# Turning softmax rows: from TensorE transposes to 32x32 block transposes on VectorE and a pass through DRAM

## The chip, the cores and the metric

The kernel runs on one core of a Trainium2 chip. A core has TensorE (PE, with its weight loads shown as PEld), VectorE (DVE), ScalarE (ACT), GpSimd (POOL) and SyncE (SP), which here only issues DMAs. Each engine works through its own instruction list in order; between engines there are only semaphores. The metric is the device time of one execution in microseconds (us): the median of the runs. One execution was also profiled, and its trace is what the views below are taken from.

## What is computed

One layer of a bidirectional encoder block, for 256 positions and a model width of 2048, in float32:

```
xn = rms_norm(x, norm_pre_w);  z = xn @ w_in
u, g_lru, q, k, v, g_attn, m_lru, m_attn = split(z)
u   = centred_depthwise_conv(u)                      # width 4
h   = rg_lru(u, forward) + rg_lru(u, backward)       # gates, decays, scans
y_a = h * silu(g_lru)
q, k = partial_rope(q), partial_rope(k)
y_b = windowed_gqa(q, k, v, sink) * silu(g_attn)     # 16 heads, 4 key/value heads, |i-j| <= 128
merged = sigmoid(m_lru) * (y_a @ w_proj_a) + sigmoid(m_attn) * (y_b @ w_proj_b)
out = x + rms_norm(merged @ w_out, norm_post_w)
```

The change touches the attention. For a head, `p = softmax(q k^T + mask, with a sink)` is a 256 x 256 matrix. It is made with the queries on the partitions, since the sums run over the keys; the product `p @ v` contracts over the keys, so TensorE wants p with the keys on the partitions. Each head's p must be turned.

## The kernel before

**Matmuls.** Every float32 factor is split into a high part (a cast to fp32r, on ScalarE) and a low part (the rest, a subtraction on VectorE); a product is three fp32r matmuls, high x high, high x low and low x high (`mm3`, lines 223 to 227). `parts_of` (line 147) does that split for activations, `split` (line 209) for weights.

**Weights and half-steps.** `START`, `MERGE` and `OUT` (lines 57 to 68) write out by hand in which order the weight blocks are used: 182 steps, each with a load of 2048 columns, treated in two halves. The loop at the end (line 1121) goes through them. Time in the program is counted in half-steps ("ticks"): a block of kind `blk` or `quad` takes two, a `part` (of the seven-product scheme `Seven`) one. One half-step is about 2.7 us of matmuls. At a step the load three steps ahead is issued on SP into one of three `raw` buffers (`fetch`, line 201, issue on line 207); at a half the weights four halves ahead are split (lines 217 to 221). All else is hung into this order by `at(tick, function)` and `soon(function)`, which is "one half-step later"; the functions due at a half-step are emitted before its matmuls. So on each engine work of the weights and work of the heads stand in one list, in the order of half-steps.

**What else SP issues.** Finished units that are not needed for a while are parked in DRAM (`park`, line 792, issue on line 797) and brought back (`back`, line 799, issue on line 801); the sums of the seven-product scheme are stored (line 335) and loaded (line 340); first cells of accumulated weights are loaded on line 194. GpSimd issues the accumulating DMAs. Buffers of 4 KB per partition come from a pool of 45 units.

**Heads.** `heads(g, b, end)` starts four heads at the ticks `b + HEADS_AT[j]`, that is b, b + 3, b + 5 and b + 8; the next group starts 11 later, and the first of all 16 half-steps before the block p0.0 of `w_proj_a`. `head` (line 859) hangs up the stages of one head, with b the head's own start: `scores` on TensorE at b; `expo` (mask and maximum on VectorE, line 877, exponentials on ScalarE) at b + 1; `normalise` at b + 3, with the scaling of p on ScalarE (line 891) one later; `flip` at b + 5: four TensorE transposes of 128 x 128 into a PSUM bank `pt` (line 897); `p_parts` at b + 6: cast to `ph` on ScalarE (line 148), subtraction to `pl` on VectorE (line 149), both from PSUM. Two heads share a pair of units: after the odd head of each pair, `values` at b + 10 multiplies v with the turned rows (six matmuls of 512 columns, lines 225 to 227, into `o`), and `gate_out` at b + 11 multiplies with the gate (line 913).

**Opening.** Lines 441 to 492: a few parameters `pv` on ScalarE's DMA queue, ten matmuls of ones on TensorE (`spin`, line 452; two instructions each, as they are plain float32), then x and the first weights in pieces on SP's queue, one piece of x on ScalarE's. The first real matmul (line 549) needs the first piece of x, scaled by `pv` on ScalarE (line 478), and the first weights, cast by VectorE (line 219).

Of the kernel before, what the change touches and what calls it, by code (L numbers as in the profile page):

```python
# [15 lines left out]
F32 = mybir.dt.float32  # L16
F32R = mybir.dt.float32r
# [4 lines left out]
P = 128  # L22
D = 2048
S = 256
# [4 lines left out]
EPS = 1e-6  # L29
UNITS = 45  # L30
DECAY = 12
SPIN = 10
HEAD0 = -16
HEADS_AT = (0, 3, 5, 8, 11)
FIRST = 8
# [42 lines left out]
PV_CW = 16  # L78
# [24 lines left out]
def content(p):  # L103
    if p[0] == "part":
        _, g, a, q = p
        m, c = SEVENS[g]
        b, f = SEVEN[a][2]
        return "part", m, c + (-512 if g == "A" else 512) * f, b, q
    return p
# [6 lines left out]
def body(ctx, tc, x, xT, wall, wlru, pvec, npost, ident_d, mask_d, rope_d, out):  # L116
    nc = tc.nc
# [5 lines left out]
    dram = ctx.enter_context(tc.tile_pool(name="dram", bufs=1, space=bass.MemoryType.DRAM))  # L123
    ctx.enter_context(tc.manual_schedule())

    def unit(name, dt=F32, shape=(P, 4, S)):
        return units.tile(list(shape), dt, tag="u", name=name)

    def bank(name, shape=(P, 2, S)):
        return psum.tile(list(shape), F32, tag="bg", name=name, bufs=4)  # L130
# [4 lines left out]
    def half_unit(name, tag, dt=F32, bufs=2):  # L135
        return small.tile([P, 2, S], dt, tag=tag, name=name, bufs=bufs)


    def pair_unit(name):
        return unit(name, F32R, (P, 2, 2, S))  # L140

    def tiny(name, n=2):
        return small.tile([P, n], F32, tag="tiny", name=name, bufs=24)
# [3 lines left out]
    def parts_of(h, l, src):  # L147
        nc.scalar.copy(h, src)  # L148
        soon(lambda: nc.vector.tensor_tensor(l, src, h.bitcast(F32), ALU.subtract))
# [9 lines left out]
    def ticks(i=None):  # L159
        return sum(1 if p[0] == "part" else 2 for p in plan[:len(steps) if i is None else i])  # L160

    def at(hs, fn):
        assert hs >= now[0], (hs, now[0])
        due.setdefault(hs, []).append(fn)
# [9 lines left out]
    def soon(fn, d=1):  # L174
        at(now[0] + d, fn)
# [6 lines left out]
    def raw_tile(i):  # L182
        t = ring.tile([P, 2, 1024], F32, tag="raw", name=f"raw{i}", bufs=3)
        raws[i] = [t[:, h] for h in range(2)]
        return t
# [12 lines left out]
    def chained(i):  # L198
        return plan[i][0] == "part" and groups[plan[i][1]].where(plan[i][2]) != "z"

    def fetch(i, lead):
        if i >= len(plan):
            return
        if plan[i][0] == "part":
            groups[plan[i][1]].fetch(plan[i], lead)
        if lead == 3 and i not in raws and not chained(i):
            nc.sync.dma_start(flat(raw_tile(i)), wall[row[content(plan[i])]])
# [15 lines left out]
    def mm3(ps, wh, wl, xh, xl, start, stop, more=False):  # L223

        nc.tensor.matmul(ps, wh, xh, start=start, stop=False, skip_group_check=more)
        nc.tensor.matmul(ps, wh, xl, start=False, stop=False, skip_group_check=more)
        nc.tensor.matmul(ps, wl, xh, start=False, stop=stop, skip_group_check=more)  # L227
# [211 lines left out]


    pv = const.tile([P, PV_N], F32, name="pv")
    nc.scalar.dma_start(pv[:, 0:PV_CW], pvec[:, 0:PV_CW])
    warm = const.tile([P, 1], F32, name="warm")
    eps = const.tile([P, 1], F32, name="eps")
    ones = const.tile([P, P], F32, name="ones")
    nc.gpsimd.memset(ones, 1.0)
    nc.gpsimd.memset(warm, 0.0)
    nc.gpsimd.memset(eps, EPS)

    spin = bank("spin", (P, 512))  # L450
    for _ in range(SPIN):
        nc.tensor.matmul(spin[:, 0:P], ones, ones, start=True, stop=True)
    norm = lambda k: pv[:, PV_NORM + k:PV_NORM + k + 1]
    ident = const.tile([P, P], F32, name="ident")
    rbc = const.tile([P, S], F32, name="rbc")

    xt = [unit(f"xT{i}") for i in range(4)]
    xs = []
    raw_tile(0)
    for j in range(4):  # L460
        (nc.scalar if j == 1 else nc.sync).dma_start(xt[0][:, j], xT[0, :, j])
        nc.sync.dma_start(raws[0][j // 2][:, j % 2 * 512:(j % 2 + 1) * 512], wall[0, :, j * 512:(j + 1) * 512])
    for i in (1, 2):
        for j in (0, 2):
# [143 lines left out]
    ab, e, den, s2, pl, rl = (const.tile([P, 32], F32, name=f"sp_{n}") for n in ("ab", "e", "den", "s2", "pl", "rl"))  # L608
# [183 lines left out]
    def park(key, store, c):  # L792

        d = parked[key, c] = dram.tile([P, 1024], F32, name=f"park{key}{c}")
        t = store[c]
        store[c] = None
        nc.sync.dma_start(d, flat(t))
# [53 lines left out]
    kv = {}  # L851
# [7 lines left out]
    def head(hd, qh, ql, b, both, end):  # L859

        g, j = hd // 4, hd % 4
        sk = pv[:, PV_SINK + hd:PV_SINK + hd + 1]
        ts = [slice(t * P, (t + 1) * P) for t in range(2)]
        v = {}

        def scores():
            v["sc"] = bank(f"sc{hd}")
            for t in range(2):
                mm3(v["sc"][:, t], qh[:, j, ts[t]], ql[:, j, ts[t]], kv["kh"][:, g], kv["kl"][:, g], True, True)

        def expo():
            p = v["p"] = half_unit(f"p{hd}", ("p", "uu")[hd % 2])
            sc = v.pop("sc")
            m, nm, es = tiny(f"m{hd}"), tiny(f"nm{hd}"), tiny(f"es{hd}")
            dn = v["dn"] = tiny(f"dn{hd}")
            for t in range(2):
                nc.vector.tensor_tensor_reduce(p[:, t], sc[:, t], table["mask"][:, t], rtok_sc[:, t:t + 1], sk, ALU.add, ALU.max, m[:, t:t + 1])  # L877
            nc.vector.tensor_scalar(nm, m, -1.0, None, ALU.mult)
            soon(lambda: exps(p, nm, es, dn))

        def exps(p, nm, es, dn):
            for t in range(2):
                nc.scalar.activation(p[:, t], p[:, t], AF.Exp, bias=nm[:, t:t + 1], accum_out=dn[:, t:t + 1])
            nc.scalar.activation(es, nm, AF.Exp, bias=sk)
            v["es"] = es

        def normalise():
            dn, rd = v["dn"], tiny(f"rd{hd}")
            nc.vector.tensor_tensor(dn, dn, v["es"], ALU.add)
            nc.vector.reciprocal(rd, dn)  # L890
            soon(lambda: [nc.scalar.activation(v["p"][:, t], v["p"][:, t], AF.Copy, scale=rd[:, t:t + 1]) for t in range(2)])

        def flip():
            v["pt"] = bank(f"pt{hd}")
            for kt in range(2):
                for t in range(2):
                    nc.tensor.transpose(v["pt"][:, kt, ts[t]], v["p"][:, t, ts[kt]], ident)  # L897

        def p_parts():
            if j % 2 == 0:  # L900
                both.update({s: unit(f"p{s}{hd}", F32R, (P, 2, 2, S)) for s in "hl"})
            parts_of(both["h"][:, :, j % 2], both["l"][:, :, j % 2], v.pop("pt"))
            v.clear()

        def values():
            both["o"] = bank(f"o{hd}")
            ks = slice(g * P, (g + 1) * P)
            for kt in range(2):
                mm3(both["o"], kv["vh"][:, kt, ks], kv["vl"][:, kt, ks], both["h"][:, kt], both["l"][:, kt], kt == 0, kt == 1)

        def gate_out():
            y = sga[g][:, j - 1:j + 1]
            nc.vector.tensor_tensor(y, both["o"], y, ALU.mult)
            both.clear()
            if j == 3 and g < 2:
                soon(lambda: park("yb", sga, g), 4)

        for d, fn in ((0, scores), (1, expo), (3, normalise), (5, flip), (6, p_parts)):
            at(b + d, fn)
        if j % 2 == 1:  # L920
            at(b + 10, values)
            at(b + 11, gate_out)
            if g > 1:
                at(max(b + 12, end + hd // 2 - 4), lambda: yb_parts(hd // 2))

    def yb_parts(q):
        yb[q] = pair_unit(f"yb{q}")
        n = q % 2 * 2
        parts_of(yb[q][:, :, 0], yb[q][:, :, 1], sga[q // 2][:, n:n + 2])

    def heads(g, b, end):
        def start():
            h, l = unit(f"qh{g}", F32R), unit(f"ql{g}", F32R)
            parts_of(h, l, qs.pop(g))
            soon(lambda: back("sga", sga, g, (P, 4, S)), 6)
            for j in range(4):
                if j % 2 == 0:
                    both = {}
                head(4 * g + j, h, l, b + HEADS_AT[j], both, end)

        if g in QPARK:
            at(b - 8, lambda: back("q", qs, g, (P, 4, S)))
        at(b - 2, start)
# [111 lines left out]
    b, n = ticks(), ticks(len(plan))  # L1055
# [159 lines left out]
```

## Time and profile before

| | us |
|---|---|
| median of 3 runs (lowest, highest) | 882.88 (882.56, 884.68) |
| the profiled execution, its own time | 884.18 |
| its span, first to last instruction | 882.4 |
| PE busy | 873.4 (99%) |
| VectorE busy | 712.3 (81%) |
| ScalarE busy | 644.3 (73%) |
| DMA traffic | 243.74 MB, 276 GB/s over the span |

Busy shares are means over the whole run; the share of a stage can be quite different. The chain that ended last is followed back from the last instruction through what released each one; a piece of it gives a start, a length, an engine and a line. In lists by line, `out<-in` are the program's names with the buffer numbers left out, followed by the shapes, the count, the busy time with the mean length of one instruction in ns, and the idle time of the engine just before them with what ended it. "Landing" is the time from the issue of a DMA to its completion. The length of a matmul includes its way through the array, so neighbours overlap; in the chain they are counted from one to the next.

### The profile page before, as it was taken

To read this page: it belongs to the slowest core of one execution; us is meant where nothing else is said; L and a number is where in the kernel's file an instruction comes from. 1 tells how busy PE (TensorE), PEld (TensorE's weight loads), DVE (VectorE), ACT (ScalarE), POOL (GpSimd) and SP (SyncE) were. 2 spreads that over 40 slices of the span, in tenths; PEclk is the share of its full clock that TensorE was granted. 3 is DMA by queue.
4 is the path that set the end of the run, shared out by engine and by line. 5 is a ranking of instruction groups with operands and counts; after the bars stand their busy time and mean duration, and the time that the engine had idled before them with its cause. 6 is when DMAs were issued, how large, how long until landed. Compare 5 with 4: busy or idle time off the path is not lost.

```text
span 882.4 us, 12374 instructions
## 1 busy us (share of the span) xinstructions
PE 873.4 (99%) x4542; PEld 750.6 (85%) x4542; DVE 712.3 (81%) x959; ACT 644.3 (73%) x937; POOL 72.7 (8%) x104
## 2 busy tenths in 40 slices
PE   9999999999999999999999999999999999999996
PEld 8888888888888888888888888888888888888885
DVE  6899999898797988889778778876677588777776
ACT  7679687877788796886877699965666555565654
POOL 0000001012000011100001100000001101000200
PEclk9999999999999999999999999999999999999998
DMA  9657699999959999996999975777879997999962
GB/s 326 248 199 246 205 361 243 358 334 295 333 180 286 325 282 317 303 327 211 268 360 306 308 254 215 232 292 222 236 297 320 318 301 239 303 286 393 260 165 96
DMA packets 54830, 243.74 MB, mean 276 GB/s; under 512 B 5872, under 2 KB 10736, under 8 KB 39280
## 3 DMA queue, kind: packets, MB, share of 16 engines
q1 hardware_dynamic: 42672, 200.33, 61.0%
q0 software_dynamic: 11520, 41.95, 24.4%
q10 hardware_dynamic: 576, 0.66, 0.3%
q8 instruction: 36, 0.59, 0.3%
q14 instruction: 26, 0.21, 0.1%
HBM read 228.24 MB, written 14.68 MB: 275 GB/s over the span
## 4 chain that ended last, share of the span: by engine, by line
PE 98%; DMA 0%; DVE 0%; ACT 0%; DVEq 0%; SPq 0%; issue 0%
PE ga L252 7%; PE q L252 7%; PE gl L252 7%; PE u L252 5%; PE Mm L407 4%; PE Lm L407 4%; PE Am L407 4%; PE Om L407 4%; PE Nm L407 4%; PE gl L250 3%; PE ga L250 3%; PE q L250 3%; PE u_ps L549 3%; PE u L250 3%; PE pa__6058 L272 2%; PE pa__5804 L272 2%
## 5 line engine op out<-in xcount | busy, mean ns | idle before, releaser
L221 DVE TENSOR_TENSOR wl<-raw,wh 128x1024 fp32r<-128x1024 f32 (+1 forms) x252 | 299.4, 1202 | 63.5 <-ACT wh L219 45.1
L219 ACT CAST wh<-raw 128x1024 fp32r<-128x1024 f32 (+1 forms) x251 | 253.6, 1036 | 54.5 <-DMA raw<-wall_dram 34.1
L252 PE MATMUL ga<-xs,wh 128*128 128x512 f32 x256 | 63.5, 391 | 0.0
L252 PE MATMUL q<-xs,wh 128*128 128x512 f32 x256 | 63.4, 392 | 0.0
L252 PE MATMUL gl<-xs,wh 128*128 128x512 f32 x256 | 63.4, 391 | 0.0
L252 PEld LDWEIGHTS gl<-xs,wh 128*128 128x128 f32 x256 | 47.0, 188 | 9.0
L252 PEld LDWEIGHTS q<-xs,wh 128*128 128x128 f32 x256 | 46.8, 188 | 8.9
L252 PEld LDWEIGHTS ga<-xs,wh 128*128 128x128 f32 x256 | 46.7, 188 | 8.8
L252 PE MATMUL u<-xs,wh 128*128 128x512 f32 x192 | 47.5, 391 | 0.0
L252 PEld LDWEIGHTS u<-xs,wh 128*128 128x128 f32 x192 | 35.2, 188 | 6.7
L250 PEld LDWEIGHTS q<-xs,wl 128*128 128x128 f32 x256 | 33.2, 191 | 1.3
L250 PEld LDWEIGHTS ga<-xs,wl 128*128 128x128 f32 x256 | 33.0, 191 | 1.2
L250 PE MATMUL q<-xs,wl 128*128 128x256 f32 x256 | 34.0, 283 | 0.0
L250 PEld LDWEIGHTS gl<-xs,wl 128*128 128x128 f32 x256 | 32.8, 191 | 1.2
L250 PE MATMUL ga<-xs,wl 128*128 128x256 f32 x256 | 33.5, 283 | 0.0
L250 PE MATMUL gl<-xs,wl 128*128 128x256 f32 x256 | 33.2, 283 | 0.0
L250 PEld LDWEIGHTS u<-xs,wl 128*128 128x128 f32 x192 | 24.6, 191 | 0.9
L250 PE MATMUL u<-xs,wl 128*128 128x256 f32 x192 | 24.9, 283 | 0.0
L654 DVE SCALAR_TENSOR_TENSOR uu<-upad,pv,uu 128x256 f32<-128x256 f32 x48 | 23.2, 483 | 1.7
L877 DVE CUSTOM_DVE_ANT_0 p<-sc,table,pv 128x256 f32<-128x256 f32 x32 | 16.1, 540 | 9.7 <-PE sc L227 9.6
L148 ACT CAST ph<-pt 128x512 fp32r<-128x512 f32 x16 | 9.3, 583 | 19.0 <-PE pt L897 19.0
L738 ACT ACTIVATE sig<-sg 128x512 f32<-128x512 f32 x16 | 10.2, 637 | 14.2 <-DVE sg L581 14.2
(503 smaller groups left out, 2104.8 us busy)
## 6 DMA issues: line engine op xcount, KB each, us to landing
raw<-wall_dram SPq DMA_DIRECT2D x121, 1024.0 KB, 7.5
lraw<-wlru_dram SPq DMA_DIRECT2D x8, 512.0 KB, 6.4
away<-xx SPq DMA_DIRECT2D x8, 512.0 KB, 8.6
Lm<-away SPq DMA_DIRECT2D x8, 512.0 KB, 13.3
Mm<-away SPq DMA_DIRECT2D x8, 512.0 KB, 13.5
Nm<-away SPq DMA_DIRECT2D x8, 512.0 KB, 14.4
Am<-away SPq DMA_DIRECT2D x8, 512.0 KB, 6.8
raw<-wall_dram SPq DMA_DIRECT2D x8, 256.0 KB, 5.0
```

The source lines that it names most:

```text
L148: nc.scalar.copy(h, src)
L219: cast(hs, raw)
L221: nc.vector.tensor_tensor(ls, raw, hs.bitcast(F32), ALU.subtract)
L250: nc.tensor.matmul(ps[:, 1], wl[:, sl], a[:, 0], start=False, stop=False)
L252: nc.tensor.matmul(ps, wh[:, sl], a, start=k == 0, stop=k == KT - 1)
L272: nc.tensor.matmul(got[t], a[:, i], (wl if low else wh)[:, sl], start=k + low + i == 0, stop=low == 1 and k == KT - 1)
L407: nc.tensor.matmul(self.ps[b], a[i], (wl if low else wh)[:, sl], start=fresh and j + low + i == 0, stop=last and j + low == 2, skip_group_ ...
L549: nc.tensor.matmul(ups[b // 2][:, b % 2, m], w[:, sl], a[:, n], start=k == 0 and w is wh and m == 0, stop=stop)
L654: nc.vector.scalar_tensor_tensor(u, up[:, j, tap:tap + S], cw[:, tap:tap + 1], u, ALU.mult, ALU.add)
L738: nc.scalar.activation(sg, dst, AF.Sigmoid)
L877: nc.vector.tensor_tensor_reduce(p[:, t], sc[:, t], table["mask"][:, t], rtok_sc[:, t:t + 1], sk, ALU.add, ALU.max, m[:, t:t + 1])
```

## The change

1. `flip` no longer uses TensorE. VectorE transposes p in blocks of 32 x 32 (one instruction for each head), into a unit `t` that two heads share. A block transpose keeps each block within its 32 partitions; what has to go between groups of 32 partitions goes by DMA.
2. `send`, one half-step after the odd head's flip: four DMAs on SP store `t` to a DRAM tensor `d`, one for each group of 32 partitions, in runs of 128 elements (512 bytes), 512 KB in all. `fetch`, two half-steps later: one DMA on SP loads `d` back into one unit, 4 KB for each partition. The stores wait for the flips, the load waits for the stores.
3. `p_parts` runs once for each pair instead of once for each head, from SBUF instead of PSUM, over 1024 elements for each partition; it stands at b + 11 of the odd head. `values` moves from b + 10 to b + 13, `gate_out` from b + 11 to b + 14; what hangs on `gate_out` (the parking of the first two groups) moves with it, while the later split of y stays at the half-step it had, as the larger of two numbers.
4. The turned rows lie in another order, so `values` reads them with a stride: 2 x 8 runs of 32 elements instead of 512 in a row.
5. In the opening, `SPIN` goes from 10 to 11; the first piece of x moves from SP's queue to the head of ScalarE's, `pv` behind it, the second piece of x third. SP's queue so begins with the first weights. Two memsets on GpSimd move behind the matmuls of ones in the program.

```diff
-SPIN = 10
+SPIN = 11
...
-    nc.scalar.dma_start(pv[:, 0:PV_CW], pvec[:, 0:PV_CW])
...
-    nc.gpsimd.memset(warm, 0.0)
-    nc.gpsimd.memset(eps, EPS)
...
         nc.tensor.matmul(spin[:, 0:P], ones, ones, start=True, stop=True)
+    nc.gpsimd.memset(warm, 0.0)
+    nc.gpsimd.memset(eps, EPS)
...
-        (nc.scalar if j == 1 else nc.sync).dma_start(xt[0][:, j], xT[0, :, j])
+        (nc.scalar if j < 2 else nc.sync).dma_start(xt[0][:, j], xT[0, :, j])
+        if j == 0:
+            nc.scalar.dma_start(pv[:, 0:PV_CW], pvec[:, 0:PV_CW])
...
         def flip():
-            v["pt"] = bank(f"pt{hd}")
-            for kt in range(2):
-                for t in range(2):
-                    nc.tensor.transpose(v["pt"][:, kt, ts[t]], v["p"][:, t, ts[kt]], ident)
+            if j % 2 == 0:
+                both["t"] = unit(f"pt{hd}", F32, (P, 2, 4, 2, 2, 32))
+            nc.vector.transpose(both["t"][:, :, :, j % 2].rearrange("p t c k x -> p t k c x"),
+                                v.pop("p").rearrange("p t (k c x) -> p t k c x", k=2, c=4))
+            v.clear()
+
+        def send():
+            d = both["d"] = dram.tile([4, 32, 2, 4, P], F32, name=f"turn{hd}")
+            t = both.pop("t")
+            for a in range(4):
+                nc.sync.dma_start(d[:, :, :, a].rearrange("c i t x -> i t c x"),
+                                  t[a * 32:(a + 1) * 32].rearrange("p t c h k x -> p t c (h k x)"))
+
+        def fetch():
+            u = both["l"] = unit(f"pl{hd}", F32R, (P, 1024))
+            nc.sync.dma_start(u.bitcast(F32), both.pop("d").rearrange("c i t a x -> (c i) (t a x)"))
 
         def p_parts():
-            if j % 2 == 0:
-                both.update({s: unit(f"p{s}{hd}", F32R, (P, 2, 2, S)) for s in "hl"})
-            parts_of(both["h"][:, :, j % 2], both["l"][:, :, j % 2], v.pop("pt"))
-            v.clear()
+            both["h"] = unit(f"ph{hd}", F32R, (P, 1024))
+            parts_of(both["h"], both["l"], both["l"].bitcast(F32))
 
         def values():
...
+            turned = [both[i].rearrange("p (a h k x) -> p h k a x", a=8, h=2, k=2) for i in "hl"]
             for kt in range(2):
-                mm3(both["o"], kv["vh"][:, kt, ks], kv["vl"][:, kt, ks], both["h"][:, kt], both["l"][:, kt], kt == 0, kt == 1)
+                mm3(both["o"], kv["vh"][:, kt, ks], kv["vl"][:, kt, ks], *(t[:, :, kt] for t in turned), kt == 0, kt == 1)
...
-        for d, fn in ((0, scores), (1, expo), (3, normalise), (5, flip), (6, p_parts)):
+        for d, fn in ((0, scores), (1, expo), (3, normalise), (5, flip)):
             at(b + d, fn)
         if j % 2 == 1:
-            at(b + 10, values)
-            at(b + 11, gate_out)
+            for d, fn in enumerate((send, None, fetch, None, None, p_parts, None, values, gate_out), 6):
+                if fn:
+                    at(b + d, fn)
             if g > 1:
-                at(max(b + 12, end + hd // 2 - 4), lambda: yb_parts(hd // 2))
+                at(max(b + 15, end + hd // 2 - 4), lambda: yb_parts(hd // 2))
```

## The prediction

> **What bounds the kernel now.** I read the page first (busy times and the chain that ended last), then TensorE's waits, then the stage of the heads, 505 to 680 us, then the first 14 us.
>
> ```profile
> span 882.4 us, 12374 instructions
> ...
> PE 873.4 (99%) x4542; PEld 750.6 (85%) x4542; DVE 712.3 (81%) x959; ACT 644.3 (73%) x937; POOL 72.7 (8%) x104
> ...
> PE 98%; DMA 0%; DVE 0%; ACT 0%; DVEq 0%; SPq 0%; issue 0%
> ```
>
> The waits of PE over the whole run (waited for, us in total, times, longest):
>
> ```profile
> PE spin L452 <- POOL eps L448: 1.0, 1, 1.0
> PE u_ps L549 <- DVE wh L219: 0.5, 1, 0.5
> ```
>
> The chain is TensorE from beginning to end, and after the first real matmul it waits for nobody. So what is taken off PE's list shortens the run by its whole length, as long as the others still deliver; and work added to VectorE, ScalarE or the DMAs costs nothing until it makes PE wait.
>
> **The turning on TensorE.** Pieces of the chain (start, length, what):
>
> ```profile
> 517.92 0.44 PE pt L897 x4
> ...
> 527.41 0.44 PE pt L897 x4
> ...
> 543.55 0.23 PE o L225
> ...
> 555.55 5.47 PE pa__5536 L272 x24
> ...
> 656.55 0.44 PE pt L897 x4
> ...
> 677.44 5.44 PE pb__6658 L272 x24
> ```
>
> Sixteen pieces of four transposes, first and last shown, are on the chain at 0.44 us each: 16 x 0.44 = 7.04 us are removed. Nothing in the heads is added to PE. The six value matmuls of a pair (0.23 each) stay, but read the turned rows in runs of 32 elements at a stride of 64; no row of this trace has such a moving operand. Its bounds are 0 and a doubling, 48 x 0.23 = 11.0 us; I take 0, since every contiguous matmul of 512 columns here runs at the same 0.23 and the element count does not change.
>
> **VectorE and ScalarE.** Costs by form in the stage of the heads (busy, mean ns | idle before):
>
> ```profile
> L221 DVE TENSOR_TENSOR wl<-raw,wh 128x1024 fp32r<-128x1024 f32 x46 | 55.9, 1220 | 10.8 <-ACT wh L219 6.1 <-PE pa__6058 L272 2.1 <-ACT yb L148 1.3
> L219 ACT CAST wh<-raw 128x1024 fp32r<-128x1024 f32 x48 | 49.2, 1045 | 7.5 <-DMA parkyb<-sga 3.1 <-DMA raw<-wall_dram 2.1 <-PE pa__6058 L272 1.9
> ...
> L149 DVE TENSOR_TENSOR pl<-pt,ph 128x512 fp32r<-128x512 f32 x16 | 10.9, 684 | 0.0
> ...
> L148 ACT CAST ph<-pt 128x512 fp32r<-128x512 f32 x16 | 9.3, 583 | 19.0 <-PE pt L897 19.0
> ...
> L838 DVE STREAM_SHUFFLE q3r<-q3r 128x256 f32<-128x256 f32 x1 | 0.4, 448 | 0.0
> ```
>
> A flip is a VectorE block transpose of 512 elements per partition, which this trace lacks. Between 512 and 1024 elements a subtraction grows by (1220 - 684) / 512 = 1.05 ns an element; the shuffle, the nearest kin, takes 448 ns for 256, so 0.45 + 256 x 1.05 ns = 0.72 us. Ends: 0.45, if it moves two elements at a time, and 1.44, if filling and draining a block do not overlap. Per pair of heads VectorE gets two flips and one subtraction of 1024 for two of 512: 1.44 + 1.22 - 1.37 = +1.29 us, over eight pairs +10.3. ScalarE gets one cast of 1024 for two of 512: 1.05 - 1.17 = -0.12, over eight pairs -1.0. Is there room?
>
> ```profile
> core 0: us, PE busy (x) PEld busy (x) DVE busy (x) ACT busy (x) POOL busy (x), PEclk, DMA share, GB/s
> 60.00:505.00 445.00, 445.00 (x2483) 390.06 (x2482) 384.68 (x471) 354.00 (x490) 42.75 (x58) 1.00 0.92 292
> 505.00:580.00 75.00, 75.00 (x406) 64.66 (x405) 61.87 (x121) 72.39 (x134) 0.00 (x0) 1.00 0.70 242
> 580.00:680.00 100.00, 100.00 (x480) 83.57 (x479) 69.73 (x116) 63.11 (x108) 6.10 (x7) 1.00 0.81 271
> ```
>
> VectorE has 13 and 30 us of air, against 4.5 and 5.8 added: hidden. ScalarE is the reader's point here: 72.4 of 75 us in the first stretch. Seven of the sixteen turns lie there, so PE wants to be through 7 x 0.44 = 3.1 us sooner, while ScalarE has 2.6 us of air plus 0.4 that the change frees. The split weights stand ahead of PE by up to four half-steps, which can carry the whole difference (loss 0), or PE meets a p_parts or a weight half that is late (loss up to 3.1). I take 1.5 lost, the middle.
>
> **The detour through DRAM.** Per pair SP issues four stores and one load more, and two waits come with them: the stores wait for the flip, the load for the stores. Behind them in SP's queue stand the weight loads of line 207, the loads of sums of line 340 and the parks and returns. The nearest rows are the stores of sums (512 KB in short runs, like the four stores together; the landing line below covers them and their loads back) and the return of a parked 512 KB, whose landing line comes second; then a weight load's row and SP's largest wait:
>
> ```profile
> L335 SPq DMA_DIRECT2D away<-xx x8: 524/525/598, 73.0 to 158.9; - x8
> ...
> DMA to landing us min/median/max: 4.0/9.2/18.2
> ```
>
> ```profile
> DMA to landing us min/median/max: 7.0/7.6/8.5
> ```
>
> ```profile
> raw<-wall_dram SPq DMA_DIRECT2D x121, 1024.0 KB, 7.5
> ```
>
> ```profile
> SPq L207 <- DVE wl L221: 435.8, 90, 15.1
> ```
>
> From the start of a flip to parts ready for PE: flip 0.72, four issues 4 x 0.525 = 2.1, landing 9.2, an issue of 0.4, landing 7.6, cast 1.05, subtraction 1.22: 22.3 us, of which 5.5 are not landings. The flip waits for the same scaled rows as the PE transposes did, so it can start about where they did. From the second head's turn to the new place of the values (half-step b + 5 to b + 13) there are 555.55 - 527.41 = 28.1 us for the first pair and, for the last, whose values go before the second half of b0.0, 677.44 + 2.72 - 656.55 = 23.6. So 5.8 and 1.3 us are to spare at median landings: cost 0, ends 0 and the first rival's. If that cover is gone, PE itself stops at the values, and what is late next is the weight half behind them.
>
> SP spends 436 us waiting for buffers of weights, so the 2.5 us of issue per pair replace waiting. A weight load that finds SP held by the load's wait starts some us later; it needs 7.5 us to land and is asked for three steps (some 14 us) ahead, so several us of delay reach the cast but not PE. The traffic: 8 x 1.05 MB = 8.4 MB, at the stage's full rate (258 GB/s at a share of about 0.76, so some 340 GB/s) 25 us of the DMAs' time in 175, raising the share to about 0.90. From 60 to 505 us it is 0.92 and PE waits for nothing.
>
> **The opening.** Instructions in order of time:
>
> ```profile
> 0.75 0.39 SPq L461 DMA_DIRECT2D xT<-xT_dram  x1
> ...
> 1.00 4.64 PE L452 MATMUL spin<-ones 128*128 128x128 f32 x20 [1.00 <-POOL eps L448]
> ...
> 1.20 0.89 SPq L462 DMA_DIRECT2D raw<-wall_dram  x2
> ...
> 3.38 0.51 ACT L478 ACTIVATE xs<-xT,pv 128x256 fp32r<-128x256 f32 x1 [0.21 <-DMA pv<-pvec_dram]
> ...
> 5.60 0.43 DVE L219 CAST wh<-raw 128x512 fp32r<-128x512 f32 x1 [5.60 <-DMA raw<-wall_dram]
> ...
> 6.17 2.05 PE L549 MATMUL u_ps<-xs,wh 128*128 128x256 f32 x8 [0.53 <-DVE wh L219]
> ...
> 8.87 1.91 PE L549 MATMUL u_ps<-xs,wh 128*128 128x256 f32 x8
> ...
> 11.09 1.11 PE L549 MATMUL u_ps<-xs,wh 128*128 128x256 f32 x8
> ```
>
> The first weights go out at 0.75 instead of 1.20, so PE could start at 6.17 - 0.45 = 5.72. One more opening matmul is two instructions of 0.23: the opening ends at 5.64 + 0.46 = 6.10 by its modelled end. The first real matmul lies between 5.72 and 6.10, I take 5.9: gain 0.3. pv moves to second on ScalarE's queue, about 0.45 later; its first reader would move from 3.38 to 3.8, long before 5.9. The moved memsets cost nothing; POOL is idle.
>
> The same matmul takes 0.24 at 8.87 and 0.14 at 11.09: near 10.6 PE begins to run about twice as fast, 4.4 us after its pause. The opening ran 4.64 us without getting there. If the pause closes, the quick pace comes between 5.7 (no uninterrupted run was quick sooner) and 5.9 + 4.4 = 10.3 (the opening counts for nothing); I take 8.0, so (10.6 - 8.0) / 2 = 1.3 us are gained, ends 0.15 and 2.4.
>
> The Trainium skill, "TensorE: Matmul & The Clock Gate", section on the HAM clock gate, says that the clock doubles after one busy window of about 3.4 us and that the windows run freely. By that rule the window from 7.2 to 10.6 was the first full one here, the quick pace would come by 7.2, and the gain would be 1.7 in place of 1.3; no row shows the windows themselves.
>
> **The sum.** The profiled execution took 884.18 us (span 882.4): 884.18 - 7.04 - 0.3 - 1.3 + 1.5 = 877.0. It stands 1.3 us above the median of the runs, 882.88, and against that the same terms give 882.88 - 7.1 = 875.7. When the quick pace comes may differ between runs and make part of that 1.3; half of it, 0.65, may so be in the quick runs already and is not gained again: 876.4.
>
> **Rivals.**
> - *The rows come back late.* The two landings together may take 28.1 - 5.5 = 22.6 us in the first pair and 18.1 in the last; medians make 16.8, the longest 26.7. PE then stands at the values of each pair. Against 7.04 / 8 = 0.9 us gained per pair it decides once landings total about 21.3 on average; at 23 it costs 2.6 x 8 = 21 us: 897. For it: the stores have shorter runs than any quoted and share the DMAs with weight loads. Against: the medians. Chance 0.10. The Trainium skill, "VectorE: DVE Perf Modes", rules for kernel authors, tells to turn 128x128 tiles on TensorE where PSUM is an acceptable destination; by that rule this rival or the next holds, and the trace has only the PE side of it, 0.44 us a head.
> - *Values read slowly.* The strided moving operand doubles 48 matmuls: 876.4 + 11.0 = 887.4. Chance 0.06.
> - *The flip is dear.* At 1.44 us the seven flips and more add 4.5 + 5.0 to 61.9 of VectorE's shortened 72 us, while it also waits for ScalarE; some 5 us come back: 881.4. Chance 0.06.
> - *The opening changes nothing*, the pause stays or the pace comes as late: 876.4 + 1.6 = 878.0. Chance 0.12.
>
> **How the numbers follow.** The forecast holds with 0.66, its own range 873.5 (nearly every term at its good end: 882.88 - 7.04 - 0.45 - 2.4 = 873.0) to 879.0 (nothing at the opening, 3.1 lost to ScalarE: 878.9). About 0.3%, 2.6 us, can be told from no change here. Faster: forecast, unchanged opening and half of the dear flip, 0.81. Within 0.3%: the other half and a mild late return, 0.06. Slower: the late return and slow values, 0.13. The range to 883 takes in the dear flip and the mild late return.
>
> **What would show it.** No pt rows on PE; PE's waits still near 1.5 us in total, with any new ones at o <- pl of VectorE or at a weight half between 540 and 600; SP waiting for the turn stores some 5 to 10 us a pair; transposes of about 0.72 on VectorE; value matmuls at 0.23; the first real matmul near 5.9 and the quick pace before 9. The prediction is wrong if PE waits over 0.9 us a pair at the values, or if those matmuls lengthen.

## The result and the profile after

| us | before | after |
|---|---|---|
| median of 6 runs each | 882.77 (882.22 to 884.68) | 879.49 (878.87 to 880.26) |
| the profiled execution, its own time | 884.18 | 880.26 |
| its span | 882.4 | 878.5 |

The ratio is 0.9956, with a 95% interval of 0.9945 to 0.9966: faster by 3.3 us, where 6.4 were forecast. The time is 0.5 us above the forecast's own range, 873.5 to 879.0; it lies only in the part up to 883 that was added for a dear flip and a mild late return of the rows, and neither came (below). That it falls in there is luck: only half of the gain came. From the page of the changed kernel: busy times and the shares of the chain that ended last.

```profile
PE 867.7 (99%) x4480; PEld 744.2 (85%) x4480; DVE 720.4 (82%) x967; ACT 643.2 (73%) x929; POOL 72.7 (8%) x104
...
PE 84%; ACT 5%; DMA 5%; issue 4%; DVE 2%; POOLq 0%; POOL 0%; ACTq 0%; DVEq 0%
```

PE's waits over the whole run (waited for, us in total, times, longest):

```profile
PE mt L982 <- DVE sm L971: 1.8, 2, 0.9
PE spin L449 <- POOL eps L451: 1.0, 1, 1.0
PE o L226 <- DVE pl L149: 0.6, 1, 0.6
```

The chain was PE from end to end. Now it runs twice through a load of weights that takes over 20 us (issued at 488.34 and at 676.88): the first leads to the wait of 0.6 us at the values, the second to a wait that nobody forecast. That one is not in the heads: line 982 turns the merged rows after the attention, on TensorE in both kernels, and line 971 is the sum that it reads. Starts of PE at the same places in the two traces, the second half of block b0.0 and then b1.0 (timelines of PE: start, length, line, operation; the first two rows are of before, the others of after):

```profile
679.99 1.07 PE L272 MATMUL pb__6658<-wh,yb 128*128 128x512 f32 x4
...
707.67 0.71 PE L272 MATMUL pb__6898<-wh,yb 128*128 128x512 f32 x2
```

```profile
672.47 1.09 PE L272 MATMUL pb__6627<-wh,yb 128*128 128x512 f32 x4
...
700.76 0.44 PE L982 MATMUL mt<-ident,sm 128*128 128x128 f32 x2 [0.91 <-DVE sm L971]
702.09 0.44 PE L982 MATMUL mt<-ident,sm 128*128 128x128 f32 x2 [0.89 <-DVE sm L971]
702.28 1.19 PE L272 MATMUL pb__6875<-wh,yb 128*128 128x512 f32 x3
```

At the second half of b0.0, behind the last values in both kernels, PE is 679.99 - 672.47 = 7.5 us ahead of before. At b1.0, some 28 us later, it is 707.67 - 702.28 = 5.4 ahead, and at the end, by the spans, 3.9. Two waits of 0.9 us take most of the first loss. The second comes right behind them: in the costs by form from 702.79 to 706.20, the products of b1.0 take 594 ns each here, and 390 in another execution of the same kernel (second row; x count, busy us, mean ns):

```profile
L272 PE MATMUL pb__6875<-wh,yb 128*128 128x512 f32 x7 | 3.2, 594 | 0.0
```

```profile
L272 PE MATMUL pb__6875<-wh,yb 128*128 128x512 f32 x11 | 3.2, 390 | 0.0
```

The granted clock in those 3.4 us is 0.50 in the first and 1.00 in the second. How the DMAs stand in the stages (columns as in the prediction; the last three are granted clock, DMA share and GB/s):

```profile
505.00:580.00 75.00, 74.41 (x389) 63.70 (x388) 65.28 (x125) 71.15 (x130) 0.00 (x0) 1.00 0.83 284
580.00:680.00 100.00, 100.00 (x459) 82.89 (x458) 79.19 (x123) 63.75 (x105) 7.84 (x9) 1.00 0.98 321
680.00:712.00 32.00, 30.20 (x130) 24.40 (x129) 18.59 (x21) 14.59 (x18) 4.37 (x5) 0.95 1.04 334
```

0.70 and 0.81 have become 0.83 and 0.98; from 680 us on the DMAs are full, as they were before:

```profile
680.00:712.00 32.00, 32.00 (x144) 26.41 (x143) 22.71 (x25) 14.57 (x17) 6.01 (x7) 1.00 1.04 321
```

And the chain of the changed kernel through the place where the gain is lost (start, length, what):

```profile
676.88 20.11 DMA raw<-wall_dram
...
699.29 0.69 DVE sm L970
702.09 0.44 PE mt L982 x2
```

A load of 1 MB takes 20.1 us to land, where the prediction had 7.5, the median of the whole run. At this place that is too little even without the change: in the kernel before the load of b1.0 took 15.0 us. Three theories follow. *Traffic*: the 8.4 MB of the detour fill the DMAs just ahead of this place, the load of b1.0 is late, and all the rest hangs on it. *Waiting*: what delays the load is SP, which holds in its queue for the stores and the load of the detour. *Pace*: the load is harmless, and what costs is the half pace that follows the two short waits.

### The profile page after: what moved, and what is told of

Its sections match the earlier page's. It is cut to its first block, busy times and chain, and to the rows that moved or that the text cites. A ratio compares the mean times of both kernels' runs of the same rounds, so it can differ in the third digit from the quotient of the medians.

```text
span 878.5 us, 12340 instructions
## 1 busy us (share of the span) xinstructions
PE 867.7 (99%) x4480; PEld 744.2 (85%) x4480; DVE 720.4 (82%) x967; ACT 643.2 (73%) x929; POOL 72.7 (8%) x104
## 4 chain that ended last, share of the span: by engine, by line
PE 84%; ACT 5%; DMA 5%; issue 4%; DVE 2%; POOLq 0%; POOL 0%; ACTq 0%; DVEq 0%
PE ga L252 7%; PE gl L252 7%; PE u L252 5%; DMA raw<-wall_dram 5%; PE Mm L407 4%; PE Lm L407 4%; PE gl L250 3%; PE ga L250 3%; PE Am L407 3%; PE Om L407 3%; PE q L252 3%; PE pb__6875 L272 3%; PE u L250 3%; PE u_ps L550 3%; PE pa__6035 L272 2%
## 5 line engine op out<-in xcount | busy, mean ns | idle before, releaser
L272 PE MATMUL pb__6875<-wh,yb 128*128 128x512 f32 x64 | 18.4, 413 | 0.0
L227 PE MATMUL gate<-ul,lwl 128*128 128x256 f32 x64 | 18.1, 283 | 0.0
```

Source lines behind the costliest of these rows:

```text
L272: nc.tensor.matmul(got[t], a[:, i], (wl if low else wh)[:, sl], start=k + low + i == 0, stop=low == 1 and k == KT - 1)
```

## The experiments

The "kernel before" was run beside each group again, with medians of 882.81, 883.02, 883.03 and 882.89 us.

**The heads without the exchange.** The flips stay, but the rows are split where they lie; no store, no load.

```diff
         def send():
-            d = both["d"] = dram.tile(...)
...
-                nc.sync.dma_start(...)
+            pass
         def fetch():
-            u = both["l"] = unit(f"pl{hd}", F32R, (P, 1024))
-            nc.sync.dma_start(...)
+            both["l"] = unit(f"pl{hd}", F32R, (P, 1024))
         def p_parts():
...
-            parts_of(both["h"], both["l"], both["l"].bitcast(F32))
+            t = both.pop("t").rearrange("p t c h k x -> p (t c h k x)")
+            parts_of(both["h"], both["l"], t)
```

> Without the four stores and the load of each pair; p_parts reads the block-transposed rows directly, so the exchange between groups of 32 partitions is left out and the rows stay only half turned. Theory (traffic): in the changed kernel the 8.4 MB through DRAM make the weight load for b1.0 late (issued 676.9, landed 697.0), and PE loses 1.8 us of waiting and 1.8 us to a half-rate stretch behind it; without them 879.5 - 3.7 = 875.8 us. Rival (queue): SP's two waits delay the weight loads, the same 875.8 here. Rival (VectorE): its added 10 us make the merged rows late; it stays at 879.5. Rival (pace): any PE that is 7 us early meets the DMA-bound stretch from 660 to 712 us; it stays at 879.5.

Measured: 877.01 us (876.53 to 877.96, 5 runs), ratio 0.9935 (0.9923 to 0.9947). PE's waits:

```profile
PE spin L449 <- POOL eps L451: 1.0, 1, 1.0
PE o L226 <- DVE pl L149: 0.2, 1, 0.2
```

The wait at the merged rows is gone. The casts of the weights of b1.0 on ScalarE tell why (first row before, second after, third this kernel; the bracket is ScalarE's idle time and what ended it):

```profile
698.82 2.00 ACT L219 CAST wh<-raw 128x1024 fp32r<-128x1024 f32 x2 [4.42 <-PE pb__6658 L272]
```

```profile
697.06 2.00 ACT L219 CAST wh<-raw 128x1024 fp32r<-128x1024 f32 x2 [2.66 <-DMA raw<-wall_dram]
```

```profile
694.06 2.00 ACT L219 CAST wh<-raw 128x1024 fp32r<-128x1024 f32 x2 [5.79 <-DMA raw<-wall_dram]
```

Before, the load was issued at 683.73 us and landed at 698.7, just when PE let ScalarE go on: it was in time, and no more. After, PE is 7.5 us earlier and the load is issued 6.9 us earlier (676.88), but it lands only 1.7 us earlier: now it ends the idle time. Without the exchange it is issued at 676.59, takes 17.4 us and lands 3.0 us sooner than with it. So by these two executions the traffic of the detour makes 2.7 of the 20.1 us. The exchange costs 879.5 - 877.0 = 2.5 us of the median, not the 3.7 expected, which counted the stretch at half pace of one execution.

**The bytes without the wait for them, and the waits without the bytes.** In the first kernel the load fetches what the pair before stored, into a unit of its own, so that it never waits for its own stores; in the second both waits stay, but 64 KB instead of 512 KB go each way.

```diff
         def fetch():
-            u = both["l"] = unit(f"pl{hd}", F32R, (P, 1024))
-            nc.sync.dma_start(u.bitcast(F32), both.pop("d")...)
+            u = both["f"] = unit(f"pf{hd}", F32, (P, 1024))
+            kept.append(both.pop("d"))
...
+                nc.sync.dma_start(u, kept[-2]...)
...
```

```diff
         def send():
-            d = both["d"] = dram.tile([4, 32, 2, 4, P], F32, name=f"turn{hd}")
+            d = both["d"] = dram.tile([32, 4, P], F32, name=f"turn{hd}")
             for a in range(4):
-                nc.sync.dma_start(...)
+                nc.sync.dma_start(d[:, a], t[a * 32:(a + 1) * 32, 0:P])
...
         def fetch():
...
+            nc.sync.dma_start(u[0:32, 0:512].bitcast(F32), both.pop("d")...)
...
```

> All the bytes, but the load of a pair fetches what the pair before had stored (the first a piece of weights), so SP does not wait for stores just issued; the heads therefore get other rows than their own. Traffic: unchanged, 879.5. Queue: with the wait for the stores gone, most of the 3.7 us come back, 876 to 877. VectorE and pace: 879.5.

> Both waits on SP and the five issues of a pair stay, but the stores and the load move 64 KB each instead of 512 KB; p_parts reads the block-transposed rows directly (the exchange is left out), its subtraction still waits for the load. Traffic: 875.8. Queue: 879.5. VectorE and pace: 879.5.

Measured: 879.53 us (878.5 to 881.96, 9 runs), ratio 0.9963 (0.9952 to 0.9975), with all bytes; 877.2 us (876.73 to 877.68, 5 runs), ratio 0.9935 (0.9922 to 0.9948), with few. PE's longest wait in the one with all bytes stands below; in the one with few PE does not wait at the merged rows at all.

```profile
PE mt L990 <- DVE sm L979: 2.0, 2, 1.1
```

So it is the bytes, and not SP's waiting: taking the wait away gains nothing, taking the bytes away gains all that leaving the exchange out does, to 0.2 us.

**The traffic in the kernel before.** The kernel before with two loads of 512 KB more in each pair, which nobody reads.

```diff
+        def spend():
+            x = unit(f"x{hd}", F32, (P, 1024))
+            nc.sync.dma_start(x, wall[hd // 2, :, 1024:2048])
...
         if j % 2 == 1:
+            at(b + 6, spend)
+            at(b + 8, lambda: nc.sync.dma_start(unit(f"y{hd}", F32, (P, 1024)), wall[hd // 2, :, 0:1024]))
             at(b + 10, values)
```

> The kernel before with two added loads of 512 KB of weights for each pair of heads, into units that nobody reads, at the half-steps of send and fetch: the traffic without the turn, PE as late as before. If it takes traffic and an early PE together, this is hidden: 882.8, within 0.5. If the traffic alone costs, 884 to 886, with PE waiting at the first turns of the merged rows as in the changed kernel.

Measured: 882.77 us (882.11 to 884.61, 11 runs), ratio 0.9998 (0.9989 to 1.0007). As many bytes cost nothing while PE is late; they fill the DMAs nearly as much (shares 0.80 and 0.91 in the two stages of the heads, against 0.83 and 0.98). The load of b1.0 suffers here too: it takes 17.5 us and lets its cast start at 700.86, 2.0 us later than before. But the first of the sums still waits for PE's products and not for weights (VectorE):

```profile
703.69 0.69 DVE L961 TENSOR_TENSOR sm<-pb__6690,sm 128x512 f32<-128x512 f32 x1 [0.52 <-PE pb__6690 L272]
```

Of the 3.55 us that VectorE stood idle there in the kernel before, 0.52 are left. What hurts is bytes and an early PE together. The gain takes away the very slack in which its traffic was to hide.

**Half pace.** Four matmuls of ones stand ahead of each of the two turns of merged rows 0, meant to keep PE busy while it would wait.

```diff
             ps = bank(f"mt{c}{i}")
+            if c == 0:
+                for _ in range(4):
+                    nc.tensor.matmul(ps[:, 0, 0:P], ones, ones, start=True, stop=True)
```

> The changed kernel with four matmuls of ones ahead of each of the first two turns of merged rows (mt of the first column block), written into the bank that the turn then overwrites: some 0.9 us each, in the place where PE waited 0.9 us twice. If the half-rate stretch of 3.4 us behind that wait comes from PE's pause, it is gone: 879.5 - 1.8 = 877.7. If it comes from something else, the fillers take the place of waiting and nothing changes, 879.5, and up to 881.3 in executions where PE had not waited.

Measured: 880.31 us (879.5 to 882.11, 9 runs), ratio 0.9969 (0.996 to 0.9979); no gain. PE's wait in its profile:

```profile
PE mt L985 <- DVE sm L971: 1.5, 2, 0.9
```

The edit does not reach what it was meant for. Both waits belong to the first turn, one ahead of each of its halves. The first set of ones stands ahead of the first half, where PE still waits 0.63 us; ahead of the second half, with a wait of 0.89, stands nothing; and the second set runs ahead of the second turn, where PE did not wait at all:

```profile
709.20 1.05 PE L981 MATMUL mt<-ones 128*128 128x128 f32 x8
```

There it only adds its length, which is about the 0.8 us by which this kernel is behind the changed one. In this profile the pace is whole from 700 to 712 us, and 1.5 us of waiting remain; so the run does not tell the waits from the pace. The changed kernel itself, once more, does:

> The changed kernel once more, beside the two others. Theory: 879.5 us; the two waits of 0.9 us for the softmaxed merged rows at 700 us are there again, whether or not a stretch of half pace follows them; if the stretch were what costs, a profile without it would be some 1.5 us shorter.

Measured: 879.52 us (877.46 to 881.39, 6 runs), ratio 0.9961 (0.9947 to 0.9974). Its profiled execution took 878.26 us, 2.0 less than the first one, with these waits and no stretch of half pace before the very end:

```profile
PE mt L982 <- DVE sm L971: 1.4, 2, 0.9
```

The waits are in both profiles, the half pace is not: of the twelve executions of the changed kernel three have a mean clock of 0.995, and they are the three slowest (880.26, 880.88, 881.39 us); the other nine, at 0.997 or more, took 877.46 to 879.83. By this the half pace adds to the loss in some executions and is not its cause.

**The opening alone, and the heads alone.** The kernel before with the new opening (the parts under 5 of the change), and the changed kernel with the old one.

> The kernel before with the new opening alone (first weights first on SP, eleven opening matmuls, first x and then the parameters on ScalarE's queue). In the changed trace PE stands 2.0 us earlier after the first half-step than before. Traffic: there is no added traffic, so this gain is kept, 882.8 - 2.0 = 880.8, where the kernel before really had its quick pace at 10.6 us. Pace: part of it is eaten in the DMA-bound stretch, 882 or more. Opening worth nothing: 882.8.

> The changed kernel with the opening of before. Theory (the heads carry the whole gain, the opening is made up for by the weights of half-step 7): the same as the changed kernel, 879.5 us, 879.1 to 880.0. Rival (the opening is worth the 1.3 us that its profile shows past half-step 7): 880.8 us or more.

Measured: 883.01 us (882.23 to 883.65, 11 runs), ratio 1.0001 (0.9992 to 1.0009), for the opening alone; 878.74 us (878.3 to 880.61, 5 runs), ratio 0.9959 (0.9947 to 0.9972), for the heads alone. By the median the opening is worth nothing, and by its interval not more than 0.7 us. The profile of before had misled: it caught an execution in which the quick pace came late. PE in the stretch from 8 to 12 us (count of matmuls in brackets), before, after, and the heads alone with the *old* opening:

```profile
8.00:12.00 4.00, 4.00 (x26) 4.00 (x25) 3.73 (x9) 3.30 (x7) 0.00 (x0) 1.00 0.97 358
```

```profile
8.00:12.00 4.00, 4.00 (x36) 4.00 (x35) 3.78 (x8) 3.30 (x7) 0.00 (x0) 1.00 0.92 310
```

```profile
8.00:12.00 4.00, 4.00 (x36) 4.00 (x35) 3.50 (x8) 3.54 (x8) 0.00 (x0) 1.00 1.04 388
```

The old opening reaches 36 matmuls too. In the kernel before with added traffic, also with the old opening, the pace doubles even within the matmuls of ones, which take 3.89 us for the same twenty that took 4.64, and this although PE stands idle after them:

```profile
1.00 3.89 PE L452 MATMUL spin<-ones 128*128 128x128 f32 x20 [1.00 <-POOL eps L448]
6.27 1.19 PE L549 MATMUL u_ps<-xs,wh 128*128 128x256 f32 x8 [1.38 <-DVE wh L219]
```

The Trainium skill, "TensorE: Matmul & The Clock Gate", section "What's actually happening", says that the windows of the gate run freely and that one and the same kernel so starts with a different number of slow matmuls from run to run. These rows agree, for one opening in three kernels: with the old opening the pace turned within the matmuls of ones, or before 8 us, or near 10.6.

**Part of the groups by the detour.** Groups of heads 0 and 1 (the first four pairs) by the detour, the others turned on TensorE as before; then groups 0 to 2.

```diff
+        detour = g < 2
         def flip():
+            if not detour:
+                v["pt"] = bank(f"pt{hd}")
...
+                return
...
```

> The detour for the first eight heads (groups 0 and 1, where the DMAs had air), TensorE transposes at their old half-steps for the last eight; 4.2 MB of added traffic instead of 8.4. Traffic theory: PE keeps 8 x 0.44 = 3.5 us less 0.6 of the losses seen at the values, and the stretch from 660 to 712 us is not hurt, since its backlog was built after 605 us: 882.8 - 2.9 = 879.9, no waits of PE at the turns of the merged rows (mt). If any traffic in the heads hurts: 881 to 882, with such waits.

> The detour for groups 0 to 2 (the first six pairs), TensorE turns the rows of group 3. Without any exchange the eight pairs gained 5.8 us of the median, 0.72 us each. Theory (what the traffic costs is paid once, where the weights of b1.0 are late, and the last two pairs' bytes, 625 to 650 us, are what makes them late): six pairs keep nearly all of theirs, 4.0 us, 878.8 us, and the two waits at the turns of the merged rows shrink or go. Rival (every pair's traffic costs the same, 0.31 us of its 0.72): 880.3 us, below two groups by 0.2. Rival (the engines' rates decide and not the bytes): as the changed kernel less a quarter, 880.3 us, with the waits where they were.

Measured: 880.53 us (880.38 to 880.83, 7 runs), ratio 0.997 (0.9959 to 0.9981), for two groups; 881.48 us (879.74 to 883.38, 11 runs), ratio 0.9984 (0.9975 to 0.9992), for three. In both the wait at the merged rows is gone. Two groups gain 2.5 us, somewhat less than half of the 5.8 that all pairs gain without the exchange. Three are a miss for every theory: where the detour gives over to TensorE, the mixed kernel makes a wait of its own. PE's waits, and its chain there (start, length, what):

```profile
PE pt L901 <- DVE pl L149: 1.4, 1, 1.4
```

```profile
639.85 2.35 DVE wl L221 x2
642.20 0.61 DVE pl L149
...
642.94 0.63 PE pt L901 x4
```

The turns wait for a subtraction that stands behind two splits of weights in VectorE's list. So this run does not tell where the traffic hurts; it shows the same mechanism at another place.

**Straight from SBUF to SBUF.** No DRAM: sixteen DMAs for each pair, one for each pair of partition groups, move the turned rows.

```diff
...
             for a in range(4):
...
+                for c in range(4):
+                    nc.sync.dma_start(to[c * 32:(c + 1) * 32, :, a], t[a * 32:(a + 1) * 32, :, c])
...
```

> The rows go straight from the one unit into the other by sixteen DMAs for each pair (32 partitions, two runs of 128 elements each), one for each of the block groups, and not through DRAM: half of the moved bytes, no traffic of DRAM, one wait instead of two on SP, but some 16 x 0.6 = 9.6 us of issue on SP for each pair. Traffic theory: most of the loss goes, 877 to 878. If SP's issue time counts, or small DMAs cost as much as large ones: 879.5 or above.

Measured: 900.99 us (900.69 to 904.01, 4 runs), ratio 1.021 (1.0193 to 1.0228). The issues on SP (count, and shortest, median, longest ns), PE's largest waits from 540 to 720 us, and the first stage of the heads:

```profile
L909 SPq DMA_DIRECT2D pl<-pt x128: 585/595/2433, 525.1 to 681.2; - x128
```

```profile
PE o L226 <- DVE pl L149: 4.8, 3, 2.0
PE o L225 <- ACT ph L148: 2.9, 1, 2.9
PE pb__6707 L272 <- ACT wh L219: 2.7, 1, 2.7
```

```profile
505.00:580.00 75.00, 70.93 (x361) 60.37 (x360) 62.64 (x118) 68.57 (x124) 0.00 (x0) 0.95 0.65 223
```

The DMAs are idler than before in this stage (0.65 against 0.70), but SP is not: 128 issues of 0.595 us are 76 us in one queue, and the weights stand in that queue too. From 520 to 700 us the weight loads land no slower than in the changed kernel (7.9 us at the median, 8.5 there), yet ScalarE's casts wait 52.6 us for them, where it was 16.5 in the changed kernel and 1.1 before: the loads are issued late. PE waits at the values and at weights, and in this stage the granted clock falls to 0.95.

**The late load taken out of VectorE's way.** In the changed kernel the low part of the first weights of b1.0 is made behind the four sums of merged rows 0 instead of ahead of them. Nothing else differs. (`LATE[0]` is the number of that half among all halves of weights.)

```diff
     def add_pb(c):
...
             if t == 1:
+                if c == 0:
+                    split(LATE[0], only="l")
...
-                if hs > FIRST:
+                if hs + 3 == LATE[0]:
+                    pass
+                elif hs > FIRST:
                     split(hs + 3, only="l")
```

> The changed kernel with one VectorE instruction moved: the low parts of the first weights of b1.0 (the wl of 1.22 us that waits for the late load) stand behind the four sums of the merged rows 0 instead of ahead of them. The products those sums read are done at 697.0 us in the last profile of the changed kernel, so the sums can run from there to 699.8 us, and TensorE reaches their turns at 699.7. Theory (the late load costs because it holds VectorE's queue, and the weights themselves come in time): the two waits of 0.9 us go, with them the stretches of half pace that some runs show, and the time is 879.5 - 1.8 = 877.7 us, 877.0 to 878.2. Rival (the load is late for b1.0 itself): the wait moves to the first matmul of b1.0 and the time stays 879.5 us.

Measured: 876.92 us (876.51 to 877.36, 5 runs), ratio 0.9929 (0.9915 to 0.9942). It is faster than both kernels. VectorE in the changed kernel (second execution) and in this one (start, length, line, operation, idle time before and what ended it):

```profile
697.64 1.22 DVE L221 TENSOR_TENSOR wl<-raw,wh 128x1024 fp32r<-128x1024 f32 x1 [2.51 <-ACT wh L219]
698.78 0.68 DVE L970 TENSOR_TENSOR sm<-pb__6627,sm 128x512 f32<-128x512 f32 x1
...
700.83 0.69 DVE L971 TENSOR_TENSOR sm<-tm,sm 128x512 f32<-128x512 f32 x1
```

```profile
697.45 0.69 DVE L971 TENSOR_TENSOR sm<-pb__6627,sm 128x512 f32<-128x512 f32 x1 [1.83 <-PE pb__6627 L273]
...
699.51 0.69 DVE L972 TENSOR_TENSOR sm<-tm,sm 128x512 f32<-128x512 f32 x1
700.12 2.35 DVE L222 TENSOR_TENSOR wl<-raw,wh 128x1024 fp32r<-128x1024 f32 x2
```

and PE's waits here:

```profile
PE spin L450 <- POOL eps L452: 1.0, 1, 1.0
PE o L227 <- DVE pl L149: 0.7, 1, 0.7
```

The load is as late as it was (20.0 us to land). But in the changed kernel the products that the sums read were finished at 697.0, and the first sum began only at 698.78: until 697.64 VectorE stood idle, 2.5 us, for weights that PE did not need yet, and then it split them. With the sums first PE waits for neither, the last sum ending 1.3 us sooner. The median is that of the kernel without the exchange (877.01), within the spread of the runs. So, as far as that spread tells, the whole cost of the traffic, 2.5 us, went through the order of one engine's list. The Trainium skill, "TensorE: Matmul & The Clock Gate", section "Architectural detail", says that ScalarE and VectorE take their instructions strictly first in, first out; that is what these two timelines show.

## Why the prediction was right or wrong

- **7.04 us off PE's list.** Right. No row of `pt` is left on PE, and the version with the sums first gains 882.89 - 876.92 = 6.0 us of the median, the one without the exchange 5.8.
- **1.5 us lost in the heads.** Right in size, and in part for the reason given. PE's lead over before, by the starts of the matmuls in the two traces, grows from 2.0 us in the opening (11.94 against 13.95) to 7.5 at the second half of b0.0, by 5.5 of the 7.0, so 1.5 are lost. They were put down to a full ScalarE and a late `p_parts`. One wait of 0.6 us at the values is of this kind: the chain reaches it from the load of 488.34, for most of the way from 509 to 562 us over ScalarE, then over VectorE to the subtraction (start, length, what):

```profile
561.70 0.20 ACT es L885
...
565.38 1.24 DVE pl L149
...
566.66 0.51 PE o L226
```

  Longer value matmuls (below), which the prediction had at 0, make about 0.5; the rest, some 0.4, is not assigned. That the middle between 0 and 3.1 met the size is therefore partly luck.
- **The value matmuls with a stride.** Taken as free, they are nearly so. From the tile `pl` of the changed kernel (shortest, median and longest ns; the mean before was 390):

```profile
L226 PE MATMUL o<-pl,vh x16: 399/402/506, 549.4 to 672.0; 128*128 128x512 f32 x16
...
DMA to landing us min/median/max: 3.3/7.8/10.8
```

  48 such matmuls, some 10 ns longer each, are about half a microsecond. By the letter of the prediction's last line their lengthening was a sign of being wrong; at under 3% of their length it is a small one. The rival of slow values (11 us) falls. The landing line under it is that of the load back.
- **A flip at 0.72 us.** Measured at 0.705; the dear flip falls, and VectorE's work in the heads is hidden, as said. The landing line is that of the four stores.

```profile
L898 DVE STREAM_TRANSPOSE pt<-p x16: 704/705/712, 516.6 to 646.6; 128x512 f32<-128x512 f32 x16
...
DMA to landing us min/median/max: 2.5/4.6/9.6
```

- **The detour in time.** Right. The two landings together take 4.6 + 7.8 = 12.4 us at the medians, where 22.6 were to be had in the first pair and 18.1 in the last; the longest of each would make 20.4, and PE's only wait at the values is 0.6. The rows do not come back late. SP waits 5.7 us in all for the stores, not 5 to 10 a pair; its larger wait is for the flips ahead of the stores, 22.1 us.
- **The traffic at no cost: the step that failed.** "From 60 to 505 us it is 0.92 and PE waits for nothing" argued from the mean share of another stage. The size of the traffic was right (q1 moves 8.3 MB more; the share rises by 0.13 and 0.17), its price was not: 2.5 us of the median (3.6 in the profiled execution, 7.5 ahead at b0.0 and 3.9 at the end), of the 3.1 us by which the result missed 876.4. The reckoning took the stage of the heads for closed, and gave a weight load 7.5 us to land, the median of the whole run. But the DMAs are full from 680 us on already before (share 1.04), the load of b1.0 took 15.0 us there and came just in time, and PE comes there 7.5 us sooner, 5.5 of them from the heads. That "several us of delay reach the cast but not PE" was true for the matmuls of b1.0 and wrong for what stands behind the split in VectorE's list.
- **The opening.** Forecast at 0.95 us net (0.3 and half of 1.3); worth 0 (ratio 1.0001). The first matmul at 5.79 was foretold (5.9), by other means: pv lands later, and the scaling of x starts at 5.23 instead of 3.38, not 3.8. The quick pace did come before 9. But it does in executions of the old opening too, once even before 4.9 us (added traffic), where the prediction had 5.7 as the earliest. And the early pace does not last as a lead: with the opening alone PE is 2.3 us ahead of the trace of before at 11.69 us and 1.2 at 29.44. The rival "the opening changes nothing" holds. The prediction took 1.6 us off for the opening and added 0.65 back, half of what the profiled execution stood above the median; with an opening worth nothing all 1.6 had to go back.

The terms, mended: 882.8 - 7.04 + 1.5 = 877.3 without the traffic's price, against 877.0 and 876.9 measured, and 877.3 + 2.5 = 879.8 with it, against 879.5.

## What to carry to other kernels

When a change takes time off the engine that bounds a kernel, everything behind it has to come sooner by as much: look past the stage that is changed, for the next place where loads land just in time, and ask which engine's list holds still for them. Here a share of the DMAs near one cost nothing until a late load stood ahead of other work in an in-order list; and moving one instruction was worth as much as taking the traffic away. And a profile of one execution can carry an accident of that execution (here 1.3 us of slow pace at the start), which is not to be counted as the change's gain.

## What was not expected of the hardware

Two waits of PE of 0.9 us, with 0.44 us of work between, were followed by 3.4 us at a granted clock of 0.50 in some executions and not in others. A mean clock under 0.997 is taken here as the mark of such an execution (the profiled one with the half pace has 0.995, the one without it 0.998). Among kernels with these two waits it shows in 3 of 12 (the changed kernel), 1 of 9 (all bytes, no wait for them), 0 of 5 (the heads alone) and 0 of 9 (with the matmuls of ones). With three groups, where PE waits once for 1.4 us, it shows in 5 of 11, and those five are the slowest (881.86 to 883.38 us; the other six 879.74 to 881.48). Where the profile has no such waits in the middle of the run (without the exchange, with few bytes, two groups, opening alone, added traffic, sums first) it shows in none of 44, and in 1 of 67 executions of the kernel before that were run beside them. So the short waits may well bring the half pace about, but no run sets it by itself; and why the nine executions of the changed kernel at full clock still spread over 2.4 us stays open. Beside that: 32-partition copies within SBUF cost SP 0.595 us of issue each, as much as a store of four times the bytes (0.610).
